# Diagonal sums of the recurrent heads: four 512-column products with a broadcast column of ones in place of eight 128-row blocks

## The chip, the core and the metric

The kernel runs on one core of one Trainium2 chip. The metric is the device time of one execution in microseconds (us). A core has a matrix engine (PE, with its weight loads shown apart as PEld), a vector engine (DVE), an activation engine (ACT), a general engine (POOL) and a queue engine that issues most transfers (SP). [...]

## The reference, cut to what matters

One decoder layer on 1024 tokens of width 1024. A projection feeds eight heads of dilated attention and four heads of a gated recurrence (HGRN2) of width 128; then follow the output projection and a feed-forward net of width 4096. The change lies in the recurrence, which the reference computes in chunks:

```python
qf = silu(q)                      # per head, (tokens, 128)
log_f = logaddexp(log(lb), log1p(-lb) + log_sigmoid(f_pre))
kf = -expm1(log_f)                # 1 - f
# in a chunk: b = cumsum(log_f)
a[t, s] = sum_k qc[t, k] * kc[s, k] * exp(b[t, k] - b[s, k])   # s <= t
o = o_inter + a @ vc
```

On the diagonal, s = t, the decay is one, and `a[t, t]` is the plain sum over the 128 channels of `qf * kf` at token t. These diagonal sums are what the changed lines compute.

## The kernel before, in words

Everything is held turned: channels on the 128 partitions, 1024 tokens along the free side. Where f32 exactness matters and speed too, a value is split in two fp32r parts (`hi` by an ACT copy, `lo = x - hi` by a DVE subtraction, `split_into` L82 to L84), and a product is done in three passes (`three_pass`, L86 to L89).

The order of the work is written by hand. A queue holds generators (projections of the next head, `hgrn_ig` L351 and `hgrn_qf` L368; in the last head the first attention projections, `attn_proj` L611). `fill(ns)` (L170) takes pieces from this queue until their stated costs have used up `ns`; so the instruction streams of all engines are a fixed weave of one head's recurrence (`hgrn_core`, L427) and the next head's projections. Debt is carried from one `fill` to the next. In front of each head's core the queue is drained.

`hgrn_qf(h)` makes, in two halves of 512 tokens, `qt` (silu of q), the forget gate `tot`, `kt` = 1 - f, and `prod = qt * kt` (L399), and then scales `qt` by `tot` (L400). DVE does these on L394 to L400, with sigmoids from ACT (L395, L396).

`hgrn_core(h)` for heads 0 to 2: `quarter_sets` (L403) makes query sets for the first step, by ACT copies (L414, L418) and DVE products (L419, L421). After `fill(3300)` come eight products `pd` (L434), one for each block of 128 tokens: the block of `prod` is the stationary operand, the column `ones` (128 x 1) the moving one, and the sums come out with tokens on the partitions, one column per block. DVE copies the 128 x 8 result (`dg`, L436) and multiplies it with the identity into `at` (L438), the matrix of diagonals that holds the scores of a head. After another `fill(1200)` come three steps. Each makes score products `pl` in four banks of the tags `s` and `t` (L451), rescales `qt`, `kt` and the totals on DVE (L464 to L478) while it makes the next query sets, and copies the scores into `at` under masks (`copy_predicated`, L483), which sets the four banks free; then `fill(7000)`. Then follow the transposed keys (`pk`), the state products (`pu`) and the outputs (`po`, two banks of the tag `pv`), and gate products of L573 that read `po`. Head 3 instead goes through seven levels, each with one bank of products `pl` (L512), DVE rescaling (L516, L518, L522) and one masked copy (L523), with fills of 2900 times 1.15.

In head 3 two things stand in front of the core (L1003 to L1005): the load of the first attention bias table, `load_bias(0)` (L691), and a dummy activation `texp` that makes ACT load its table for the exponential ahead of time. The rows of weights are split by `w_split` (L107), called as pieces of the queue are taken; its lines in the profile are L83 (ACT, `wh`) and L84 (DVE, `wl`).

Buffers go round in rings by tag: `S` nine slabs of 128 x 1024, `BT` two, `half` two of 128 x 512; in PSUM two banks each for `mm`, `s`, `t` and `pv`. `prod` was a slab of `S`, `pd` a bank of `t`. `BT` is used by the attention's bias tables and later by weights.

Of the kernel before, what the change touches and what calls it, by code (L numbers as in the profile page):

```python
# [8 lines left out]
F32 = mybir.dt.float32  # L9
F32R = mybir.dt.float32r  # L10
U8 = mybir.dt.uint8
AF = mybir.ActivationFunctionType
ALU = mybir.AluOpType
# [4 lines left out]
P = 128  # L18
# [3 lines left out]
NT = T // P  # L22
# [4 lines left out]
HH = 4  # L27
# [3 lines left out]
def f32(ap):  # L31
    return ap.bitcast(F32)
# [3 lines left out]
def hymba_layer(ctx, tc, x, w_in, w_out, w_ff1, w_ff2, g_pre, lb_logits, g_mix, g_post,  # L36
                g_mlp, g_mlp_post, bias_tab, level_masks, ident_in, fold_in, out):
    nc = tc.nc
    V, S, G, TE = nc.vector, nc.scalar, nc.gpsimd, nc.tensor

    ctx.enter_context(tc.manual_schedule())
    cp = ctx.enter_context(tc.tile_pool(name="consts", bufs=1))
# [7 lines left out]
    def slab(tag, name, dtype=F32, shape=(P, T)):  # L50
        return sp.tile(list(shape), dtype, tag=tag, name=name,
                       bufs={"S": 9, "T": 9, "P": 3, "BT": 2, "V8": 2, "R": 1}[tag])

    def bank(tag, name):
        return ps.tile([P, 512], F32, tag=tag, name=name,
                       bufs={"mm": 2, "s": 2, "t": 2, "pv": 2}[tag])

    def half(name, dtype=F32):
        return sp.tile([P, 512], dtype, tag="half", name=name, bufs=2)

    def col(name, n=1):
        return tp.tile([P, n], F32, tag=f"c{n}", name=name)

    ident = cp.tile([P, P], F32, name="ident")
# [3 lines left out]
    lbl = cp.tile([P, HH, 2], F32, name="lbl")  # L68
    lb = cp.tile([P, HH], F32, name="lb")
    omlb = cp.tile([P, HH], F32, name="omlb")  # L70
    ones = cp.tile([P, 1], F32, name="ones")
    nhalf = cp.tile([P, NT], F32, name="nhalf")
    rstd0 = cp.tile([P, NT], F32, name="rstd0")
    ssq0 = cp.tile([P, NT], F32, name="ssq0")
# [32 lines left out]
    def w_split(eng=V):  # L107
        i = done[1]
        if i < len(stream):
            if done[0] <= i:  # L110
                w_load()
            hl = stream[i][1]
            if hl is None:
                hl = (wp.tile([P, T], F32R, tag="wh", name=f"wh{i}", bufs=2),
                      wp.tile([P, T], F32R, tag="wl", name=f"wl{i}", bufs=2))
            else:
                hl = hl()
            split_into(hl[0], hl[1], raws.pop(i), eng)
            parts[i] = hl
            done[1] += 1  # L120
            w_load()

    def w_get(i, ahead=1):
        while done[1] < min(i + 1 + ahead, len(stream)):
            w_split()
        return parts[i]
# [43 lines left out]
    def fill(ns, least=False):  # L170
        debt[0] += ns
        if least:
            debt[0] = max(debt[0], 1.0)
        while debt[0] > 0 and queue:
            try:
                cost = next(queue[0])
            except StopIteration:
                queue.pop(0)
                continue
            if cost is None:  # L180
                break
            debt[0] -= cost
        debt[0] = min(debt[0], 0.0)

    def drain():
        while queue:
            n = len(queue)
            fill(1e9)
            assert len(queue) < n or not queue
# [20 lines left out]
    def x_load(t):  # L210
        nc.sync.dma_start(out=xrows[t], in_=x[t * P:(t + 1) * P, :])
# [5 lines left out]
    for c in range(2):  # L217
        sl = slice(c * 512, c * 512 + 512)
# [4 lines left out]
            nc.sync.dma_start(out=raws[i][:, sl], in_=stream[i][0][:, sl])  # L223
    for t in range(1, NT):
        x_load(t)
    V.memset(ones, 1.0)
    V.memset(nhalf, -0.5)
    rrow = slab("R", "rrow")
    mraw = slab("T", "mraw", F32, (P, len(LEVELS), 64))
# [46 lines left out]
    def row_scale(hf):  # L276
        sl = slice(hf * 512, hf * 512 + 512)
        pt = bank("t", f"rb{hf}")
        for j in range(4):
            t = hf * 4 + j  # L280
            TE.transpose(pt[:, j * P:(j + 1) * P], rstd0[:, t:t + 1].to_broadcast([P, P]), ident)
        S.activation(rrow[:, sl], pt, AF.Copy)
# [44 lines left out]
    for q in (2, 3):  # L327
# [7 lines left out]
                    in1=first.unsqueeze(2).to_broadcast([P, 3, 64]), op=ALU.mult)  # L335
# [5 lines left out]
    def proj_t(w, name, hf, out_box):  # L341
        wh, wl = kc(w[0]), kc(w[1])
        pm = bank("mm", f"pm_{name}{hf}")
        for k in range(NK):
            three_pass(pm, (wh[:, k], wl[:, k]), part(hT, k, hf), k == 0, k == NK - 1)
            out_box[0] = pm
            if k < NK - 1:
                yield 650.0
# [19 lines left out]
    def hgrn_qf(h):  # L368
        hd = heads[h]
        box = [None]  # L370
        w = w_get(4 * h + 2)
        hd["prod"] = slab("S", f"prod{h}")
        qt = hd["qt"] = slab("S", f"qt{h}")
        sig = slab("P", f"sig{h}")
        for hf in range(2):
            sl = slice(hf * 512, hf * 512 + 512)
            yield from proj_t(w, f"q{h}", hf, box)
            if h == 0:
                row_scale(hf)
            V.tensor_tensor(out=qt[:, sl], in0=box[0], in1=rrow[:, sl], op=ALU.mult)  # L380
            S.activation(sig[:, sl], qt[:, sl], AF.Sigmoid)
            V.tensor_tensor(out=qt[:, sl], in0=qt[:, sl], in1=sig[:, sl], op=ALU.mult)
            yield 650.0
        w = w_get(4 * h + 3, 0)
        kt = hd["kt"] = slab("S", f"kt{h}")
        tot = hd["tot"] = slab("S", f"tot{h}")
        for hf in range(2):
            sl = slice(hf * 512, hf * 512 + 512)
            for n, cost in enumerate(proj_t(w, f"f{h}", hf, box)):
                if hf == 0 and n == 3:  # L390
                    w_get(4 * h + 3, 2 if h + 1 < HH else 1)
                yield cost
            fr = half(f"fr{h}{hf}")
            V.tensor_tensor(out=fr, in0=box[0], in1=rrow[:, sl], op=ALU.mult)  # L394
            S.activation(tot[:, sl], fr, AF.Sigmoid)  # L395
            S.activation(kt[:, sl], fr, AF.Sigmoid, scale=-1.0)  # L396
            V.tensor_scalar(tot[:, sl], tot[:, sl], omlb[:, h:h + 1], lb[:, h:h + 1], op0=ALU.mult, op1=ALU.add)
            V.tensor_scalar(kt[:, sl], kt[:, sl], omlb[:, h:h + 1], None, op0=ALU.mult)
            V.tensor_tensor(out=hd["prod"][:, sl], in0=qt[:, sl], in1=kt[:, sl], op=ALU.mult)  # L399
            V.tensor_tensor(out=qt[:, sl], in0=qt[:, sl], in1=tot[:, sl], op=ALU.mult)  # L400
            yield 650.0

    def quarter_sets(hd, h, step, tots):  # L403
# [23 lines left out]
    def hgrn_core(h, scale, after=None):  # L427
        hd = heads[h]
        inat, gate, prod, qt, kt, tot = (hd[n] for n in ("inat", "gate", "prod", "qt", "kt", "tot"))
        ready = quarter_sets(hd, h, 0, tot) if h < HH - 1 else None  # L430
        fill(3300 * scale)
        pd = bank("t", f"pd{h}")
        for c in range(NT):
            TE.matmul(pd[:, c:c + 1], prod[:, c * P:(c + 1) * P], ones, start=True, stop=True)  # L434
        dg = col("dg", NT)
        V.tensor_copy(dg, pd[:, :NT])  # L436
        at = slab("S", f"at{h}", F32, (P, NT, P))
        V.tensor_tensor(out=at, in0=ident.unsqueeze(1).to_broadcast([P, NT, P]),  # L438
                        in1=dg.unsqueeze(2).to_broadcast([P, NT, P]), op=ALU.mult)
        if h < HH - 1:  # L440
            fill(1200 * scale)
            totals = slab("P", f"tot{h}")
            for step in range(3):
                c = 4 ** step
# [3 lines left out]
                for u in range(4):  # L448
                    pl = bank("st"[u // 2], f"pl{h}_{step}{u}").rearrange("p (n q) -> p n q", n=2)
                    for n in range(2 * u, 2 * u + 2):  # L450
                        TE.matmul(pl[:, n % 2, :192], kt[:, n * P:(n + 1) * P], sets[u // 2][:, n % 4],  # L451
                                  start=True, stop=True)
# [12 lines left out]
                for hf in range(2):  # L465
# [3 lines left out]
                                    in0=sets[hf][:, :, 128:].rearrange("p n (b w) -> p n b w", b=nb),  # L469
                                    in1=cv[:, n4, :, 0:1].to_broadcast([P, 4, nb, 2 * c]), op=ALU.mult)  # L470
# [19 lines left out]
            for n in range(NT):  # L490
                TE.matmul(pl[:64, n * 64:(n + 1) * 64], kt[:, n * P:n * P + 64], qt[:, n * P + 64:(n + 1) * P],
                          start=True, stop=True)
# [8 lines left out]
            fill(3400 * scale)  # L501
        else:
            cur = tot
            fill(1200 * scale)
            for li, c in enumerate(LEVELS):
                nb = 64 // c
                qv = qt.rearrange("p (b two c) -> p b two c", two=2, c=c)
# [3 lines left out]
                for n in range(NT):  # L511
# [5 lines left out]
                                in1=cv[:, :, 1:2].to_broadcast([P, w, c]), op=ALU.mult)  # L517
                V.tensor_tensor(out=qv[:, :, 1, :], in0=qv[:, :, 1, :],  # L518
                                in1=cv[:, :, 0:1].to_broadcast([P, w, c]), op=ALU.mult)
# [10 lines left out]
        for hf in range(2):  # L530
            pt = bank("t", f"pk{h}_{hf}")
            for j in range(4):
                n = hf * 4 + j
# [4 lines left out]
        for g4 in range(2):  # L538
            pu = bank("pv", f"pu{h}_{g4}")
            for j in range(min(4, NT - 1 - g4 * 4)):  # L540
                n = g4 * 4 + j
                TE.matmul(pu[:, j * P:(j + 1) * P], ktr[:, n], inat[:, n], start=True, stop=True)
            for j in range(min(4, NT - 1 - g4 * 4)):
                n = g4 * 4 + j
# [10 lines left out]
        for g4 in range(2):  # L555
            po = bank("pv", f"po{h}_{g4}").rearrange("p (n c) -> p n c", n=4)
            for j in range(4):
                n = g4 * 4 + j
# [132 lines left out]
    def load_bias(hd):  # L691
        if hd < AH and hd not in bts:
            bts[hd] = slab("BT", f"bt{hd}") if hd < AH - 1 else early["table"][:, 0]
            nc.sync.dma_start(out=bts[hd], in_=bias_tab[hd])
# [305 lines left out]
    for h in range(HH):  # L1000
        last = h == HH - 1
        queue += [attn_proj(0), attn_proj(1)] if last else [hgrn_ig(h + 1), hgrn_qf(h + 1)]
        if last:  # L1003
            load_bias(0)
            S.activation(col("texp"), nhalf[:, :1], AF.Exp)  # L1005
        hgrn_core(h, 1.15 if last else 1.0, open_attention if last else None)
        if not last:
            drain()
# [23 lines left out]
    for s in range(n_steps):  # L1032
        if s % 16 == 6:
            first_done[s // 16] = True
        hd, b = steps[s]
# [731 lines left out]
    scale, base = gpre, lbl.rearrange("p h l -> p (h l)")  # L1767
# [95 lines left out]
    for i in range(4):  # L1863
        t = 4 + i
# [100 lines left out]
```

## Time and profile before

| what | us |
|---|---|
| median of 3 runs (lowest, highest) | 1245.24 (1244.72, 1245.63) |
| the profiled execution | 1245.78 |
| its span, first to last instruction | 1244.0 |
| PE busy, 62 to 312 us (the four heads' cores) | 247.67 of 250 |
| DVE busy, same stretch | 179.64 |
| ACT busy, same stretch | 71.69 |
| POOL busy, same stretch | 15.26 |

The profile is of one execution. In its rows, a time is the start since the first instruction, then the duration, the engine, the line of the kernel, the operation, the output and its inputs, the shape, and in brackets the idle time ahead of it with whom it waited for. Matmuls are pipelined: the next one starts before the last has ended, so the distance between starts is what one costs. A plain-f32 matmul shows as two records: the eight products of one head are sixteen records.

### The profile page before, as it was taken

How to read it: one execution, taken by the hardware profiler on the slowest of the kernel's cores; microseconds unless marked ns; L12 is line 12 of the kernel's file. 1: busy time of each engine (PE TensorE's matmuls, PEld its weight loads, DVE VectorE, ACT ScalarE, POOL GpSimd, SP SyncE). 2: the span in 40 equal slices, each digit the busy share in tenths (PEclk: the TensorE clock that was granted, in tenths of full speed). 3: DMA queues.
4: the chain of work that ended last, by engine and by line, in shares of the span. 5: the costliest groups of instructions: out<-in, count | busy, mean ns of one | idle time of the engine just before them, and what ended most of it. 6: DMA issues, size and time to landing. Idle time of an engine off the chain costs nothing. (4 is left out here: it accounts for less than half of the span.)

```text
span 1244.0 us, 17240 instructions
## 1 busy us (share of the span) xinstructions
PE 1228.6 (99%) x6510; PEld 1051.1 (84%) x6510; DVE 865.3 (70%) x1490; ACT 543.4 (44%) x995; POOL 308.7 (25%) x304
## 2 busy tenths in 40 slices
PE   8999999999999999999999999999999999999998
PEld 8898989888888888888878788888888888888886
DVE  5686959584766667768769766676678645388795
ACT  7623232222655556665565322222225453444462
POOL 0000000020312123146250477557532000000022
PEclk9999999999999999999999999999999999999999
DMA  5201111121313233345342546455378624433337
GB/s 213 69 18 51 35 52 35 35 85 52 102 53 101 56 98 110 105 143 177 104 151 79 209 169 237 161 203 186 126 290 312 233 89 160 162 87 99 119 101 272
DMA packets 61138, 159.75 MB, mean 128 GB/s; under 512 B 5248, under 2 KB 13184, under 8 KB 61056
## 3 DMA queue, kind: packets, MB, share of 16 engines
q1 hardware_dynamic: 61056, 158.66, 37.9%
q8 instruction: 51, 0.84, 0.3%
q14 instruction: 31, 0.25, 0.1%
HBM read 110.40 MB, written 41.94 MB: 122 GB/s over the span
## 5 line engine op out<-in xcount | busy, mean ns | idle before, releaser
L84 DVE TENSOR_TENSOR al<-ar,ah 128x1024 fp32r<-128x1024 f32 x56 | 70.6, 1261 | 79.5 <-ACT ah L83 77.0
L1705 PE MATMUL f<-bh,al 128*128 128x512 f32 x320 | 124.5, 389 | 0.0
L1705 PE MATMUL f<-bh,ah 128*128 128x512 f32 x320 | 124.5, 389 | 0.0
L1705 PE MATMUL f<-bl,ah 128*128 128x512 f32 x320 | 124.5, 389 | 0.0
L83 ACT ACTIVATE ah<-ar 128x1024 fp32r<-128x1024 f32 x56 | 59.1, 1056 | 87.6 <-DMA ar<-actd 85.3
L1705 PEld LDWEIGHTS f<-bh,ah 128*128 128x128 f32 x320 | 60.1, 188 | 12.6
L1705 PEld LDWEIGHTS f<-bh,al 128*128 128x128 f32 x320 | 60.1, 188 | 12.6
L1705 PEld LDWEIGHTS f<-bl,ah 128*128 128x128 f32 x320 | 60.1, 188 | 12.3
L745 DVE TENSOR_TENSOR ptl<-pt,pth 128x512 fp32r<-128x512 f32 (+2 forms) x96 | 50.3, 552 | 20.0 <-ACT pth L744 19.9
L1779 POOL TENSOR_SCALAR lbl<-ssq 128x1 f32<-128x1 f32 x4 | 3.3, 818 | 244.4 <-ACT fd L1775 244.3
L744 ACT ACTIVATE pth<-pt 128x512 fp32r<-128x512 f32 (+2 forms) x96 | 43.3, 486 | 39.9 <-PE pt L741 38.7
L717 DVE CUSTOM_DVE_ANT_0 p<-ps,bt 128x512 f32<-128x512 f32 (+2 forms) x84 | 44.4, 553 | 22.1 <-PE ps L715 21.8
L1332 POOL TENSOR_TENSOR e<-x,e 128x512 f32<-128x512 f32 x14 | 21.5, 1539 | 134.1 <-DVE x L1283 134.1
L774 POOL TENSOR_TENSOR anat<-anat,rd 128x128 f32<-128x128 f32 x32 | 16.4, 512 | 150.0 <-DVE anat L773 147.4
L728 ACT ACTIVATE p<-p,nm 128x128 f32<-128x128 f32 (+3 forms) x64 | 49.5, 773 | 6.9 <-DVE nm L721 6.5
L79 POOL TENSOR_SCALAR ms<-hss 128x8 f32<-128x8 f32 x4 | 0.8, 197 | 199.9 <-DVE hss L564 199.8
L1705 PE MATMUL f2s<-bl,ah 128*128 128x512 f32 (+1 forms) x128 | 48.9, 382 | 0.0
L1705 PE MATMUL f2s<-bh,al 128*128 128x512 f32 (+1 forms) x128 | 48.9, 382 | 0.0
L1705 PE MATMUL f2s<-bh,ah 128*128 128x512 f32 (+1 forms) x128 | 48.9, 382 | 0.0
L741 PE MATMUL pt<-ident,p 128*128 128x128 f32 x288 | 42.7, 275 | 0.9 <-DVE ptl L745 0.7
L84 DVE TENSOR_TENSOR bl<-br,bh 128x1024 fp32r<-128x1024 f32 x32 | 40.1, 1253 | 1.3 <-ACT bh L83 1.2
L758 PE MATMUL pov<-pth,v 128*128 128x256 f32 (+1 forms) x160 | 40.3, 287 | 0.0
(1634 smaller groups left out, 3935.3 us busy)
## 6 DMA issues: line engine op xcount, KB each, us to landing
ar<-actd SPq DMA_DIRECT2D x56, 512.0 KB, 3.6
br<-in_w_ff_dram SPq DMA_DIRECT2D x16, 1024.0 KB, 6.2
w1r<-in_w_ff_dram SPq DMA_DIRECT2D x14, 1024.0 KB, 6.3
raw<-in_w_in_dram SPq DMA_DIRECT2D x26, 512.0 KB, 3.5
actd<-e SPq DMA_DIRECT2D x17, 768.0 KB, 4.1
actd<-e SPq DMA_DIRECT2D x11, 1024.0 KB, 4.0
raw<-in_w_out_dram SPq DMA_DIRECT2D x8, 512.0 KB, 3.6
xres<-in_x_dram SPq DMA_DIRECT2D x8, 512.0 KB, 4.2
```

Source lines behind the costliest of these rows:

```text
L83: S.activation(hi, src, AF.Copy)
L84: eng.tensor_tensor(out=lo, in0=src, in1=f32(hi), op=ALU.subtract)
L717: V.tensor_tensor_reduce(out=pe[:, k0:k0 + n], in0=pS[:, :n], in1=bts[hd][:, o:o + n], scale=1.0, scalar=-3.0e38, op0=ALU.add, op1=ALU.max ...
L728: S.activation(pe[:, :nk], pe[:, :nk], AF.Exp, bias=nm[:, b:b + 1], accum_out=dn[:, b:b + 1])
L741: TE.transpose(pt[:, j * P:(j + 1) * P], pe[:, jj * P:(jj + 1) * P], ident)
L744: S.activation(hi, src, AF.Copy)
L745: V.tensor_tensor(out=lo, in0=src, in1=f32(hi), op=ALU.subtract)
L758: TE.matmul(po[:, c0:256], vst, pt[j // 4][q][:, j % 4, c0:], start=j == 0 and q == 0, stop=j == nj - 1 and q == 1)
L774: G.tensor_tensor(out=dst, in0=dst, in1=stats[hd]["rd"][:, b].unsqueeze(2).to_broadcast([P, 2, 64]), op=ALU.mult)
L1332: eng[0].tensor_tensor(out=e1[:, 3], in0=a21, in1=e1[:, 2], op=ALU.add)
L1705: TE.matmul(pm, a[:, j, c], b[:, j, d], start=start and j == 0 and q == 0, stop=stop and j == 1 and q == 2, skip_group_check=True)
L1779: G.tensor_scalar(base[:, t:t + 1], sums[j][:, t:t + 1], 1.0 / D, EPS, op0=ALU.mult, op1=ALU.add)
```

## The change

The stationary and the moving operand change places: the column of ones, broadcast to 128 x 128, is loaded as weights, and the product runs past it as 512 moving columns. Each row of the bank then holds the same 512 sums, and the identity picks the diagonal out of it. So that this runs in fp32r, the product is split: `full` in f32 (a `half` buffer), `prod[0]` its ACT copy in fp32r, `prod[1]` the rest by a DVE subtraction; the bank takes two passes. Per head there are four matmuls of 512 columns in place of eight of one column, two ACT copies and two DVE subtractions more, two diagonal products of 128 x 512 on DVE that read PSUM in place of one of 128 x 1024 and a small copy. `prod` moves from one slab of `S` to both of `BT`, `pd` from a bank of `t` to the two of `pv`. The two fills become one of 4500 ahead of the products. The load of the first bias table moves behind the products of head 3, since it takes a `BT` slab.

```diff
-    ones = cp.tile([P, 1], F32, name="ones")
+    ones = cp.tile([P, 1], F32R, name="ones")
...
-    V.memset(ones, 1.0)
+    V.memset(f32(ones), 1.0)
...
     def hgrn_qf(h):
-        hd["prod"] = slab("S", f"prod{h}")
...
         w = w_get(4 * h + 3, 0)
+        hd["prod"] = prod = [slab("BT", f"pr{q}{h}", F32R) for q in "hl"]
         kt = hd["kt"] = slab("S", f"kt{h}")
...
             V.tensor_scalar(kt[:, sl], kt[:, sl], omlb[:, h:h + 1], None, op0=ALU.mult)
-            V.tensor_tensor(out=hd["prod"][:, sl], in0=qt[:, sl], in1=kt[:, sl], op=ALU.mult)
+            full = half(f"pr{h}{hf}")
+            V.tensor_tensor(out=full, in0=qt[:, sl], in1=kt[:, sl], op=ALU.mult)
+            S.activation(prod[0][:, sl], full, AF.Copy)
             V.tensor_tensor(out=qt[:, sl], in0=qt[:, sl], in1=tot[:, sl], op=ALU.mult)
+            V.tensor_tensor(out=prod[1][:, sl], in0=full, in1=f32(prod[0][:, sl]), op=ALU.subtract)
             yield 650.0
...
     def hgrn_core(h, scale, after=None):
-        fill(3300 * scale)
-        pd = bank("t", f"pd{h}")
-        for c in range(NT):
-            TE.matmul(pd[:, c:c + 1], prod[:, c * P:(c + 1) * P], ones, start=True, stop=True)
-        dg = col("dg", NT)
-        V.tensor_copy(dg, pd[:, :NT])
+        fill(4500 * scale)
         at = slab("S", f"at{h}", F32, (P, NT, P))
-        V.tensor_tensor(out=at, in0=ident.unsqueeze(1).to_broadcast([P, NT, P]),
-                        in1=dg.unsqueeze(2).to_broadcast([P, NT, P]), op=ALU.mult)
+        for hf in range(2):
+            pd = bank("pv", f"pd{h}_{hf}")
+            for q in range(2):
+                TE.matmul(pd, ones.to_broadcast([P, P]), prod[q][:, hf * 512:hf * 512 + 512], start=q == 0, stop=q == 1)
+            V.tensor_tensor(out=at[:, hf * 4:hf * 4 + 4], in0=ident.unsqueeze(1).to_broadcast([P, 4, P]),
+                            in1=pd.rearrange("p (n c) -> p n c", n=4), op=ALU.mult)
+        if h == HH - 1:
+            load_bias(0)
         if h < HH - 1:
-            fill(1200 * scale)
             totals = slab("P", f"tot{h}")
...
         else:
             cur = tot
-            fill(1200 * scale)
             for li, c in enumerate(LEVELS):
...
         if last:
-            load_bias(0)
             S.activation(col("texp"), nhalf[:, :1], AF.Exp)
```

## The prediction

> **What bounds the kernel now.** I read the page first, then the waits of the recurrent heads, then the timelines of the engines around the changed lines. The page's engine lines (busy time, share of the span, instructions):
>
> ```profile
> span 1244.0 us, 17240 instructions
> PE 1228.6 (99%) x6510; PEld 1051.1 (84%) x6510; DVE 865.3 (70%) x1490; ACT 543.4 (44%) x995; POOL 308.7 (25%) x304
> ```
>
> PE is busy for 99% of the span, so at first sight any PE time removed comes off the end. But this is a mean over stages. The windows view gives head 1's stretch from the last projection to the end of its second set of score products (columns: window, length, then busy us of PE, PEld, DVE, ACT, POOL):
>
> ```profile
> 125.20:146.50 21.30, 20.35 (x154) 19.39 (x154) 19.59 (x45) 6.86 (x20) 0.00 (x0) 1.00 0.16 50
> ```
>
> There DVE is busy 19.59 of 21.30 us, nearly as much as PE. The waits of 40 to 320 us (total, times, longest) say who waits:
>
> ```profile
> DVE kt L476 <- PE pl L451: 6.8, 3, 2.3
> ...
> PEld pl L451 <- DVE at L483: 4.7, 8, 0.6
> ```
>
> PE's weight loads for `pl` wait eight times for the masked copies of L483, which free the score banks. In the third step of each head it is DVE that waits for PE (L476, three times, up to 2.3 us): PE is the later one again by then, so what DVE costs PE in step 1 is neither won back nor paid a second time. The PEld timeline of head 1:
>
> ```profile
> 128.72 1.88 PEld L434 LDWEIGHTS pd<-ones,prod 128*128 128x128 f32 x16
> 130.52 0.19 PEld L87 LDWEIGHTS pig<-wig2h,hTh 128*128 128x128 f32 x1
> ...
> 131.94 2.59 PEld L451 LDWEIGHTS pl<-qs,kt 128*128 128x128 f32 x16
> ...
> 145.90 0.62 PEld L451 LDWEIGHTS pl<-qs,kt 128*128 128x128 f32 x4 [0.61 <-DVE at L483]
> ```
>
> The diagonal products occupy PE from 128.72 to 130.52, 1.80 us. PE's last bank of step 1 starts at 145.90 only because DVE has just finished with it. The DVE timeline that leads there:
>
> ```profile
> 119.92 0.69 DVE L564 TENSOR_REDUCE hss<-ysq 128x4 f32<-128x512 f32 x1 [2.43 <-ACT ysq L563]
> ...
> 123.67 0.69 DVE L400 TENSOR_TENSOR qt<-qt,tot 128x512 f32<-128x512 f32 x1
> 124.28 2.15 DVE L573 SCALAR_TENSOR_TENSOR gate<-po,hrs,gate 128x128 f32<-128x128 f32 x8
> 126.35 0.68 DVE L394 TENSOR_TENSOR fr<-pm_f,rrow 128x512 f32<-128x512 f32 x1
> ...
> 128.77 0.69 DVE L399 TENSOR_TENSOR prod<-qt,kt 128x512 f32<-128x512 f32 x1
> 129.50 0.69 DVE L400 TENSOR_TENSOR qt<-qt,tot 128x512 f32<-128x512 f32 x1
> 130.11 0.38 DVE L419 TENSOR_TENSOR qs<-qt,tot 128x128 f32<-128x128 f32 x1
> ...
> 131.43 0.43 DVE L421 TENSOR_TENSOR qs<-qs,tot 128x256 f32<-128x256 f32 x1
> 131.97 1.23 DVE L84 TENSOR_TENSOR wl<-raw,wh 128x1024 fp32r<-128x1024 f32 x1
> 133.11 0.16 DVE L436 COPY dg<-pd 128x8 f32<-128x8 f32 x1
> ...
> 134.45 0.62 DVE L464 TENSOR_TENSOR qt<-qt,tot 128x256 f32<-128x256 f32 x1
> ...
> 145.41 0.44 DVE L483 COPY_PREDICATED at<-near,pl 128x128 f32<-128x128 uint8 x1
> ```
>
> DVE starts this chain when PE lets it (the 2.43 us wait for `ysq`, whose source is PE's `po`), and from there to 145.85 it has no gap but short ones in which ACT works for it. So between those two points time is DVE's chain, not PE's sum. The last masked copy ends at 145.41 + 0.44 = 145.85, and PE's bank starts 0.05 later.
>
> **The change part by part.** PE first. Pitch, not duration, is what a matmul costs in a stream; here is one of the projection, fp32r, 512 columns:
>
> ```profile
> 59.27 0.39 PE L87 MATMUL pm_f<-hTh,wh 128*128 128x512 f32 x1
> 59.50 0.39 PE L88 MATMUL pm_f<-hTl,wh 128*128 128x512 f32 x1
> ```
>
> Four new ones per head cost 4 x 0.23 = 0.9 us for the 1.8 us removed: PE saves 0.9 us per head, 3.6 us in four. The weight load of a broadcast column I take as hidden behind the stream, as the other loads are; it can be no dearer than the loads it replaces, since there are four and not sixteen.
>
> DVE and ACT next. The split adds, per half, one ACT copy and one DVE subtraction. The nearest rows have their very shapes:
>
> ```profile
> L83 ACT ACTIVATE wf<-s 128x512 fp32r<-128x512 f32 x14 | 8.7, 621 | 1.3 <-POOL e L1334 1.2
> ```
> ```profile
> L84 DVE TENSOR_TENSOR wig0l<-raw,wig0h x4: 683/692/693, 6.3 to 10.9; 128x512 fp32r<-128x512 f32 x4
> ```
>
> The copy (0.62) runs beside the scaling of `qt` (0.69), so the subtraction starts some 0.06 us after `qt` and then pushes what follows by its pitch of 0.61 (129.50 to 130.11): 0.67 us per half. The diagonal itself gets slightly cheaper: column copy and product took 133.11 to 134.45 = 1.34; two 128x512 products at 0.61 are 1.22, so -0.12. Before L84 DVE idles a little (131.43 + 0.43 = 131.86 to 131.97), since ACT's `wh` is not there:
>
> ```profile
> 130.89 1.04 ACT L83 ACTIVATE wh<-raw 128x1024 fp32r<-128x1024 f32 x1
> ```
>
> ACT is delayed by about as much as DVE, less the second half's copy being over early, so I let that 0.11 be given back.
>
> Heads 1 and 2: the first half's subtraction stands ahead of the eight gate products of L573, and L394 starts right behind those (124.28 + 2.07), so 0.67 passes through; the second half adds 0.67. Sum 1.34 - 0.12 - 0.11 = **+1.1 us each** at 145.85, hence at PE. The 0.9 us that PE saves before it is spent waiting in step 1. PE meets new waits on the way, the `pl` of step 0 among them (its operands from L421 come 1.3 later, about 0.4 us after PE gets there), but these hide in the same wait.
>
> Head 0: the first half costs nothing, because DVE waits there for PE:
>
> ```profile
> 62.87 0.69 DVE L394 TENSOR_TENSOR fr<-pm_f,rrow 128x512 f32<-128x512 f32 x1 [1.51 <-PE pm_f L89]
> ```
>
> That leaves 0.67 - 0.12, about **+0.5**. Head 3 has no quarter steps and works level by level. ACT's, DVE's, POOL's and PEld's timelines:
>
> ```profile
> 255.11 1.28 ACT L1005 ACT_TABLE_LOAD   x1
> 256.40 0.20 ACT L1005 ACTIVATE texp<-nhalf 128x1 f32<-128x1 f32 x1
> 256.51 1.04 ACT L83 ACTIVATE wh<-raw 128x1024 fp32r<-128x1024 f32 x1
> ```
> ```profile
> 255.65 0.69 DVE L399 TENSOR_TENSOR prod<-qt,kt 128x512 f32<-128x512 f32 x1
> ...
> 261.32 0.69 DVE L516 TENSOR_TENSOR kt<-kt,tot 128x512 f32<-128x512 f32 x1 [0.57 <-PE pl L512]
> 261.93 1.78 DVE L518 TENSOR_TENSOR qt<-qt,tot 128x512 f32<-128x512 f32 x1
> ```
> ```profile
> 261.49 3.37 POOL L629 TENSOR_TENSOR ql<-qf,q 64x512 fp32r<-64x512 f32 x2 [11.66 <-ACT q L628]
> ```
> ```profile
> 255.98 1.98 PEld L434 LDWEIGHTS pd<-ones,prod 128*128 128x128 f32 x16
> 259.16 1.98 PEld L512 LDWEIGHTS pl<-qt,kt 128*128 128x128 f32 x16
> 265.06 1.98 PEld L512 LDWEIGHTS pl<-qt,kt 128*128 128x128 f32 x16
> ```
>
> The second half's product moves to 256.32, its ACT copy runs 257.05 to 257.65, and the table load, which stood right behind the sigmoids, now stands behind that copy: `wh` ends at about 260.05 instead of 257.55. DVE waits for it, then does `wl` (1.14), the attention query's evacuation (0.61), two diagonal products (1.22): L516 starts at 263.1 instead of 261.32. PE has two more projection steps before `pd` (six matmuls at 0.23, to 257.35), waits there for the second half's subtraction (257.7 to 258.4), starts the first `pl` at 258.7 instead of 259.16 and would reach the second at 264.6 instead of 265.06. It needs L518. With L516 and L518 at 0.61 and 1.70, as before, that is 265.4. But POOL's subtractions move with the evacuation to about 262.7 to 266.0, and what DVE runs beside them took 1.78 instead of 0.69; now L516 is caught as well, and L518 ends near 266.3. I take 266.3, **+1.2** for PE; the bounds are -0.9 (no wait at all) and +1.5 (both at full 1.78).
>
> Moved buffers: `prod` leaves S for BT, idle until the bias tables, and the bias load now waits for `pd`, behind the next weight load in SP's queue. Its first use is in the attention stage, after all seven levels of head 3; queued behind it are the copies of the query's low part, which wait for POOL's L629 anyway: nothing. The two `pv` banks of `pd` are free once L573 ends (126.4), ahead of 128.72: nothing; were that cover gone, the wait would again fall in DVE's shadow.
>
> Sum: 0.5 + 1.1 + 1.1 + 1.2 = +3.9 us. The profiled execution took 1245.78 us, 1.78 around its span, and would take 1249.7; it lies 0.54 above the median of the three runs, 1245.24, on which the forecast stands: **1249.1 us**.
>
> [...]
>
> **Rivals.** *A, faster: PE is the bound everywhere.* DVE has a hole in each half, while ACT makes the sigmoid (eight halves):
>
> ```profile
> DVE tot L397 <- ACT tot L395: 5.6, 8, 0.7
> ```
>
> If the new work falls into such holes and the chain gets shorter, PE keeps 0.9 x 4: 1245.24 - 3.6 = 1241.6. It decides once the last copy of step 1 comes 0.9 us sooner than now. For it: 99% PE. Against: the eight waits on L483, and a DVE queue that runs in order, so that a subtraction can't slide back into a hole. [...]
>
> *B, about the same: head 3 gains.* If the table load slips ahead, or POOL doesn't hold L516 up, head 3 gives 0 to -0.9 and the total is 2.7 - 0.5 = +2.2: 1247.4.
>
> *C, a hold behind the table load* as long as the load itself (1.28): head 3 is 1.3 later, 1250.4.
>
> *D, the new products aren't fast.* Were they run at the plain-f32 rate of `pl` (2.59 us for eight of 192 columns, 0.86 per 512), four would take 3.5 us, 1.7 more than those removed. Heads 0 to 2 would hide nearly all of it in step 1's wait, head 3 not: about 1251. Against it: both operands are fp32r, as in the projection.
>
> **How the numbers follow.** Forecast 0.55, A 0.13, B 0.22, C 0.05, D 0.05. About 0.2% (2.5 us) is what a measurement of this kernel can tell from no change: faster is A, 0.13; same is B, 0.22; slower is the rest, 0.65. The forecast's own range is 1247.8 to 1249.8: head 3 between +0.2 and +1.5, heads 0 to 2 between 2.4 and 3.1 (five subtractions at 0.61, or at 0.69 + 0.06). Upward the range goes to 1250.6 to take in C; downward it goes past B to 1244.3, where DVE's chain would be neither longer nor shorter and head 3 had its 0.9; it leaves out A, and D's upper part.
>
> **What would show it.** In the changed profile: four `pd` matmuls per head some 0.23 apart (else D); L483's waits by L451 longer, and in heads 0 to 2 from the first bank on (else A); the second `pl` of head 3 waiting for L518, with L516 near 1.7 us (else B). I am wrong if PE reaches step 1 after DVE, or if the ACT copy is so late that DVE stands still for it.

## The result and the profile after

| | median, us | runs | lowest to highest |
|---|---|---|---|
| before | 1245.64 | 6 | 1244.72 to 1246.05 |
| changed | 1250.78 | 6 | 1248.93 to 1251.35 |

The ratio is 1.0044, with a 95% interval of 1.0034 to 1.0054: the change makes the kernel slower by some 5.1 us. The forecast, 1249.1, had the direction; the measured time lies 0.2 us above the upper end of its range, 1250.6. The profiled execution took 1250.63, with a span of 1248.8.

The page of the changed kernel, engine lines and the row of the clock that PE was granted (tenths, 40 slices):

```profile
span 1248.8 us, 17160 instructions
PE 1230.5 (99%) x6462; PEld 1049.8 (84%) x6462; DVE 865.8 (69%) x1498; ACT 548.3 (44%) x1003; POOL 307.9 (25%) x304
...
PEclk9999999989999999999999999999999999999999
```

PE is busy for 1.9 us more, though its work per head became shorter; and in the ninth slice, about 250 to 281 us, where head 3 lies, the clock row has an 8. Before the change it had none. The waits of 40 to 330 us:

```profile
PEld pl L454 <- DVE at L486: 6.9, 12, 0.6
...
PEld pl L514 <- issue: 1.9, 1, 1.9
...
PE pl L514 <- DVE qt L520: 1.6, 1, 1.6
```

PE's weight loads now wait twelve times, not eight, for the masked copies (L486 is the old L483), and there is a new wait, nearly two us in one piece, at the second level of head 3 (L514 is the old L512). PEld of head 1, the same rows as in the prediction:

```profile
129.95 0.19 PEld L439 LDWEIGHTS pd<-prh,ones 128*128 128x128 f32 x1
130.07 0.19 PEld L439 LDWEIGHTS pd<-prl,ones 128*128 128x128 f32 x1
130.64 0.18 PEld L439 LDWEIGHTS pd<-prh,ones 128*128 128x128 f32 x1 [0.38 <-ACT prh L401]
131.36 0.18 PEld L439 LDWEIGHTS pd<-prl,ones 128*128 128x128 f32 x1 [0.54 <-DVE prl L403]
132.19 2.57 PEld L454 LDWEIGHTS pl<-qs,kt 128*128 128x128 f32 x16 [0.65 <-DVE qs L424]
142.96 0.62 PEld L454 LDWEIGHTS pl<-qs,kt 128*128 128x128 f32 x4 [0.56 <-DVE at L486]
...
146.65 0.62 PEld L454 LDWEIGHTS pl<-qs,kt 128*128 128x128 f32 x4 [0.61 <-DVE at L486]
```

The four products cost no more than their place in the stream where nothing holds them up (in head 0 they start at 67.17, 67.41, 67.63 and 67.87), but here PE waits for their operands, for the query sets behind them, and then from the first bank of step 1 on. DVE of head 1:

```profile
119.71 0.69 DVE L566 TENSOR_REDUCE hss<-ysq 128x4 f32<-128x512 f32 x1 [2.43 <-ACT ysq L565]
...
123.46 0.69 DVE L402 TENSOR_TENSOR qt<-qt,tot 128x512 f32<-128x512 f32 x1
124.13 0.69 DVE L403 TENSOR_TENSOR prl<-pr,prh 128x512 fp32r<-128x512 f32 x1
124.73 2.15 DVE L575 SCALAR_TENSOR_TENSOR gate<-po,hrs,gate 128x128 f32<-128x128 f32 x8
...
132.90 1.22 DVE L84 TENSOR_TENSOR wl<-raw,wh 128x1024 fp32r<-128x1024 f32 x1
134.03 1.28 DVE L440 TENSOR_TENSOR at<-ident,pd 128x512 f32<-128x512 f32 x2
135.23 0.62 DVE L467 TENSOR_TENSOR qt<-qt,tot 128x256 f32<-128x256 f32 x1
```

From DVE's start (L564, now L566) to PE's last bank of step 1 it was 145.90 - 119.92 = 25.98 us; now it is 146.65 - 119.71 = 26.94: **+0.96**. This measure, DVE's start to PE's last bank in head 1, is used for every kernel below. Set side by side instruction by instruction, the two traces give +0.25 for head 0 and +0.94 for head 2. Head 3, by ACT, DVE, POOL and PEld, in this order:

```profile
258.75 0.63 ACT L401 ACTIVATE prh<-pr 128x512 fp32r<-128x512 f32 x1 [1.28 <-DVE pr L400]
259.40 1.28 ACT L1006 ACT_TABLE_LOAD   x1
260.69 0.20 ACT L1006 ACTIVATE texp<-nhalf 128x1 f32<-128x1 f32 x1
260.80 1.04 ACT L83 ACTIVATE wh<-raw 128x1024 fp32r<-128x1024 f32 x1
```
```profile
261.88 1.23 DVE L84 TENSOR_TENSOR wl<-raw,wh 128x1024 fp32r<-128x1024 f32 x1 [1.77 <-ACT wh L83]
...
264.81 1.48 DVE L518 TENSOR_TENSOR kt<-kt,tot 128x512 f32<-128x512 f32 x1
266.21 1.75 DVE L520 TENSOR_TENSOR qt<-qt,tot 128x512 f32<-128x512 f32 x1
```
```profile
264.44 2.97 POOL L631 TENSOR_TENSOR ql<-qf,q 64x512 fp32r<-64x512 f32 x2 [13.25 <-ACT q L630]
```
```profile
260.27 1.98 PEld L514 LDWEIGHTS pl<-qt,kt 128*128 128x128 f32 x16
...
268.08 2.67 PEld L514 LDWEIGHTS pl<-qt,kt 128*128 128x128 f32 x16 [1.95 <-issue]
...
276.39 1.98 PEld L514 LDWEIGHTS pl<-qt,kt 128*128 128x128 f32 x16
```

This is the forecast chain to the step: the table load behind the copy, the weights' split behind the load, L518 and L520 slowed beside POOL, PE waiting 1.95 us. But then the third level starts 8.31 us after the second, where before the change it was 5.24 (265.06 to 270.30):

```profile
270.30 1.87 PEld L512 LDWEIGHTS pl<-qt,kt 128*128 128x128 f32 x15
```

The windows view around that place shows why (the last numbers are granted clock, share and rate of transfers):

```profile
262.00:269.00 7.00, 5.45 (x30) 4.40 (x30) 7.00 (x8) 1.26 (x2) 2.89 (x2) 1.00 0.39 107
269.00:275.80 6.80, 6.80 (x22) 5.74 (x22) 4.20 (x6) 1.31 (x3) 0.66 (x1) 0.50 0.28 83
275.80:283.00 7.20, 7.20 (x47) 6.41 (x46) 3.92 (x6) 1.00 (x1) 1.89 (x2) 1.00 0.24 43
```

PE's clock was **halved for 6.8 us**, right after the wait, and PE did 22 matmuls there where the next 7.2 us hold 47. That cost 3.1 to 3.3 us, and the forecast has no such term. Together, instruction against instruction in the two profiled executions: -0.46 at the start of the program (the first transfers), +0.25, +0.96, +0.94, +1.13 in the heads, +3.26 by the clock, and -1.26 behind them (at the start of the attention and of the feed-forward, where the other execution waited): 4.82, the difference of the spans.

The 6.8 us hold for the profiled execution, whose mean granted clock is 0.996. By themselves they bring the mean over 1249 us down to 0.9973. Four of the other five runs (1250.30 to 1251.35) show 0.998 and the one of 1248.93 shows 0.999, so in these the clock was down for a shorter time or not at all. What each of them lost by it was not traced.

### The profile page after: what moved, and what is told of

Read it like the earlier page. It is cut to its first block, busy times and chain, and to the rows that moved or that the text cites. A ratio compares the mean times of both kernels' runs of the same rounds, so it can differ in the third digit from the quotient of the medians.

```text
span 1248.8 us, 17160 instructions
## 1 busy us (share of the span) xinstructions
PE 1230.5 (99%) x6462; PEld 1049.8 (84%) x6462; DVE 865.8 (69%) x1498; ACT 548.3 (44%) x1003; POOL 307.9 (25%) x304
## 5 line engine op out<-in xcount | busy, mean ns | idle before, releaser
L84 DVE TENSOR_TENSOR al<-ar,ah 128x1024 fp32r<-128x1024 f32 x56 | 70.6, 1261 | 79.9 <-ACT ah L83 77.7
L84 DVE TENSOR_TENSOR bl<-br,bh 128x1024 fp32r<-128x1024 f32 x32 | 40.1, 1253 | 1.1 <-ACT bh L83 1.0
```

Source lines behind the costliest of these rows:

```text
L84: eng.tensor_tensor(out=lo, in0=src, in1=f32(hi), op=ALU.subtract)
```

## The experiments

The theory: in heads 0 to 2 DVE's chain, with ACT's part of it, sets when step 1 ends, and PE's work there counts for nothing; in head 3 a delayed split makes PE wait, and the wait halves the clock. The rivals: PE's sum counts; the lower clock belongs to the kind of work in the changed heads; the new products themselves are dear. Each kernel was timed in turn with the kernel before on the same chip; the medians of before were 1244.52 for e1 to e4, 1244.79 for e6 with four copies and 1244.81 for the rest. The times expected of e1 to e4 were reckoned from the 1245.64 of the result, so they are best read as differences from it.

**e1_texp_later.** The changed kernel, with the dummy exponential moved:

```diff
+        if h == HH - 1:
             load_bias(0)
+            S.activation(col("texp"), nhalf[:, :1], AF.Exp)
...
-        if last:
-            S.activation(col("texp"), nhalf[:, :1], AF.Exp)
```

> The changed kernel, with the dummy exponential of head 3 (and so the activation table load) issued behind the diagonal products instead of ahead of the core; nothing else is different. Theory 1 (chain and clock): in head 3 the weights' ACT split no longer stands behind the 1.28 us load, DVE's chain ends about 1.4 us sooner, PE's 1.95 us wait at the second level goes to 0.3 or less, and the half clock that followed it (6.8 us, some 3.3 us lost) does not come. Heads 0 to 2 keep their +0.3, +0.95, +0.95. Time 1246.2 to 1247.6. Theory 2 (the lower clock comes from the kind of work in the changed heads, not from the wait): the clock still falls, time 1249.5 or more. Theory 3 (the new products themselves cost PE more than those they replace): 1250 and no change in heads 0 to 2.

Measured: 1246.88 (1246.22 to 1247.91), ratio 1.0018 (1.0009 to 1.0027). Head 3's second level:

```profile
266.62 1.53 PEld L515 LDWEIGHTS pl<-qt,kt 128*128 128x128 f32 x13 [0.46 <-issue]
```

The wait fell from 1.95 to 0.46 us, where 0.3 or less was foreseen, and the clock was 1.00 throughout:

```profile
262.00:268.00 6.00, 5.93 (x34) 4.89 (x34) 6.00 (x7) 2.75 (x4) 2.92 (x2) 1.00 0.60 142
268.00:275.00 7.00, 7.00 (x43) 6.16 (x43) 4.80 (x8) 2.32 (x3) 2.15 (x2) 1.00 0.17 66
```

So about half of the 5.1 us hung on where one 1.28 us load stands in ACT's queue. Heads 0 to 2 kept their price (+0.41, +0.93, +0.94), and head 3 gains 0.36. What is left, 2.4 us, is somewhat more than the 0.6 to 2.0 expected; the next run takes it apart.

**e2_no_low.** As e1, without the low part: the DVE subtraction and the second pass are taken out.

```diff
-            V.tensor_tensor(out=prod[1][:, sl], in0=full, in1=f32(prod[0][:, sl]), op=ALU.subtract)
...
-            for q in range(2):
-                TE.matmul(pd, ones.to_broadcast([P, P]), prod[q][:, ...], start=q == 0, stop=q == 1)
+            TE.matmul(pd, ones.to_broadcast([P, P]), prod[0][:, ...], start=True, stop=True)
```

> As e1_texp_later, but the low part of the product is left out: no DVE subtraction and one pass instead of two for each bank of diagonal sums, so the sums are only fp32r-exact. Per head PE has 0.45 us less than with both passes, 1.35 less than before the change; DVE's chain is about 0.1 to 0.2 us shorter than before the change. Theory 1 (DVE's chain sets the end of step 1 in heads 0 to 2): these heads end 0.1 to 0.3 us sooner than before, PE's saving turns into wait, and only head 3 gives its 1.35. Time 1243.4 to 1244.4. Rival A of the prediction (PE's sum is the bound everywhere): 4 x 1.35 = 5.4 us off, 1240.2.

Measured: 1244.26 (1243.57 to 1245.57), ratio 0.9996 (0.9987 to 1.0005). With 5.4 us less PE work than before the change, the time is the same within the noise: rival A is refuted. But the theory's number was missed too: -0.3 us against before, where -1.2 to -2.2 was expected. In the heads ACT's half of the chain is the reason. Head 1:

```profile
130.18 0.43 DVE L423 TENSOR_TENSOR qs<-qs,tot 128x256 f32<-128x256 f32 x1 [0.31 <-ACT qs L420]
...
131.77 1.23 DVE L84 TENSOR_TENSOR wl<-raw,wh 128x1024 fp32r<-128x1024 f32 x1 [0.33 <-ACT wh L83]
```

Without its subtraction DVE waits twice for ACT, which has the copy to do first. Head 1's measure is 145.52 - 119.29 = 26.23, +0.25 and not -0.2. By these two waits it is the ACT copy that costs it, although no run has the copy alone; the two subtractions of head 1 cost the other 0.7.

**e3_no_products.** The kernel before, without the diagonal products.

```diff
-        pd = bank("t", f"pd{h}")
-        for c in range(NT):
-            TE.matmul(pd[:, c:c + 1], prod[:, c * P:(c + 1) * P], ones, start=True, stop=True)
-        V.tensor_copy(dg, pd[:, :NT])
+        V.tensor_copy(dg, prod[:, :NT])
```

> The kernel before, with the eight diagonal products of each head left out: the column copy reads eight columns of the product slab instead, so the diagonals are wrong and PE has 1.8 us less work per head while DVE has the same work. Theory 1: heads 0 to 2 end step 1 at the same time as before, PE waiting up to 1.8 us more for the masked copies; only head 3 gives 1.8. Time 1243.8, and up to 3.4 us more for each head in which that wait, now 1.8 us in one piece, halves the clock. Rival A (PE's sum): 7.2 us off, 1238.4.

Measured: 1242.75 (1242.63 to 1245.54), ratio 0.9987 (0.9979 to 0.9996), 1.8 us off. Head 1, DVE and PEld:

```profile
119.95 0.69 DVE L561 TENSOR_REDUCE hss<-ysq 128x4 f32<-128x512 f32 x1 [2.43 <-ACT ysq L560]
```
```profile
131.11 2.57 PEld L448 LDWEIGHTS pl<-qs,kt 128*128 128x128 f32 x16 [0.85 <-DVE qs L421]
142.18 0.62 PEld L448 LDWEIGHTS pl<-qs,kt 128*128 128x128 f32 x4 [0.85 <-DVE at L480]
...
145.88 0.62 PEld L448 LDWEIGHTS pl<-qs,kt 128*128 128x128 f32 x4 [0.61 <-DVE at L480]
```

The measure is 25.93, as before the change (25.98), with 1.8 us of PE work gone: PE waits 0.85 and 0.85 instead. Only head 3 gives its 1.8. This is the plainest proof that in heads 0 to 2 no saving on PE can be seen. The waits were split in two, and the clock stayed (mean 0.999 in the profiled execution, as in that of before).

The profiled execution of e3 is the slowest of its eleven, 1245.54. Against the profile of before it lost 1.7 us far behind the heads, in the feed-forward, where the split of a weight came late; below are the wait, the stretch of 3.41 us that holds nearly all of it, and the next:

```profile
640.07 0.19 PEld L1263 LDWEIGHTS f13a<-h2h,wa3l 128*128 128x128 f32 x1 [2.00 <-DVE wa3l L84]
```
```profile
636.55:639.96 3.41, 1.96 (x8) 1.05 (x6) 2.21 (x1) 3.27 (x5) 3.25 (x3) 1.00 0.13 54
639.96:643.37 3.41, 3.30 (x14) 2.74 (x15) 3.10 (x3) 1.88 (x3) 3.41 (x3) 1.00 0.00 0
```

So PE's weight loads waited 2.00 us in one piece here, and the clock stayed at 1.00 behind it. That bears on the theory of head 3 and is taken up below.

**e4_head3_only.** The old lines in heads 0 to 2, the new ones in head 3; the edit is the change itself, kept to the last head:

```diff
+        new = h == HH - 1
+        if not new:
+            hd["prod"] = slab("S", f"prod{h}")
...
+        if new:
+            hd["prod"] = prod = [slab("BT", f"pr{q}{h}", F32R) for q in "hl"]
...
+            if new:
+                S.activation(prod[0][:, sl], full, AF.Copy)
```

> The kernel before in heads 0 to 2 and the changed kernel in head 3 alone. Theory 1: head 3 waits as in the changed kernel, 1.5 to 2 us at the second level, and the clock halves for about 6.8 us: +1.1 and +3.3, less what the start of the attention gives back (0.8): 1248.7 to 1249.7. Theory 2 (the clock falls for what heads 0 to 2 did, the wait is not enough): about +1.1, 1246.7. Rival A: -0.9, 1244.7.

Measured: 1247.24 (1245.06 to 1249.11), ratio 1.0020 (1.0011 to 1.0028): between the two theories, with runs spread over four us, from next to no loss to the whole of it. Its profiled execution, of 1249.11, waited 1.93 us at the second level, and the clock fell, for one stretch of 3.4 us:

```profile
264.90:268.30 3.40, 1.86 (x15) 1.43 (x13) 3.40 (x4) 0.00 (x0) 1.55 (x1) 1.00 0.37 92
268.40:271.80 3.40, 3.40 (x13) 2.92 (x13) 2.50 (x5) 0.00 (x0) 0.00 (x0) 0.50 0.49 149
271.80:275.00 3.20, 3.20 (x21) 2.79 (x19) 1.29 (x2) 1.83 (x3) 1.17 (x1) 1.00 0.02 5
```

Heads 0 to 2 are not needed for it. The forecast of a full 6.8 us in every run was wrong. The runs' mean clocks go with their times: 0.998 in the five from 1247.74 to 1249.11, 0.999 in the six from 1245.06 to 1247.24.

**e6_late_by_3, e6_late_by_4, e6_late_by_5.** Nothing of the change: the kernel before, with idle ACT copies ahead of head 3's core (three, four, five), which delay the split of the weights and so make a wait of a chosen length.

```diff
             S.activation(col("texp"), nhalf[:, :1], AF.Exp)
+            idle = slab("P", "idle")
+            for _ in range(5):
+                S.activation(idle, rrow, AF.Copy)
```

> The kernel before with three idle ACT copies of 128x1024 (about 2.9 us) ahead of head 3's core, which only delay the split of the weights in head 3. By head 3's timeline this makes PE wait at its second level for about 2.9 - 2.0 = 0.9 us. Theory 1: that wait is paid once and the clock stays: 1244.5 + 0.9 = 1245.4. If the clock's fall belonged to any wait at this place: 1247 to 1249.

> As e6_late_by_5 with four copies. With five, PE waited 2.3 us at the second level and the clock halved for 6.8 us; with three it did not wait at all. Four should make it wait 1.1 to 1.4 us. [...]

> As e6_late_by_3 with five copies (about 4.8 us), nothing of the changed kernel in it: PE waits about 2.8 us at the second level. Theory 1 (the wait itself halves the clock): the clock falls to a half for one or two stretches of 3.4 us: 1244.5 + 2.8 + 1.7 to 3.4 = 1249.0 to 1250.7, in nearly every run. Theory 2 (the kind of work in the changed lines makes it fall): 1247.3 with a clock of 1.00 throughout.

Measured: with three 1244.94, ratio 0.9998 (0.9990 to 1.0007); with four 1246.16, 1.0012 (1.0003 to 1.0021); with five 1250.48 (1247.57 to 1251.32), 1.0036 (1.0022 to 1.0050). The second level of each, in this order (with three it has no wait: the 0.9 us foreseen was wrong, since POOL now came at 264.44 us, too late to slow L516 and L518, 0.68 and 0.69 us long):

```profile
264.94 1.92 PEld L512 LDWEIGHTS pl<-qt,kt 128*128 128x128 f32 x16
```
```profile
265.64 1.53 PEld L512 LDWEIGHTS pl<-qt,kt 128*128 128x128 f32 x13 [1.20 <-DVE qt L518]
```
```profile
267.24 2.71 PEld L512 LDWEIGHTS pl<-qt,kt 128*128 128x128 f32 x16 [2.29 <-DVE qt L518]
```

And the clock with five:

```profile
268.00:275.00 7.00, 7.00 (x24) 5.94 (x23) 5.51 (x7) 1.31 (x3) 2.58 (x3) 0.51 0.17 40
```

A wait of 2.29 us, in a kernel that has none of the changed lines, halves the clock for 6.8 us in the profiled execution, and the median is 5.7 us above before; the three slowest runs have a mean clock of 0.996 to 0.997, the others 0.998 (1248.90) and 0.999 (1247.57). With a wait of 1.20 the kernel costs 1.4 us, about what the wait lasts, and the clock stays (mean 0.999 in the profiled execution). Theory 2 is refuted: at this place it is the wait, and not the changed lines.

**e7_low_on_pool.** As e1, with the subtraction on POOL.

```diff
-            V.tensor_tensor(out=prod[1][:, sl], in0=full, in1=f32(prod[0][:, sl]), op=ALU.subtract)
+            G.tensor_tensor(out=prod[1][:, sl], in0=full, in1=f32(prod[0][:, sl]), op=ALU.subtract)
```

> As e1_texp_later, with the subtraction of the split moved from DVE to POOL (about 1.3 us for 128x512 in rows of the later stages). If DVE's own two subtractions are the cost in heads 0 to 2, and POOL beside it were free, this falls to the time of e2_no_low plus 0.45 for head 3: 1244.7. If POOL holds DVE up while both read (the 1.78 us rows of head 3), what DVE runs beside it takes some 1.0 longer per half and nothing or little is won: 1246.5 to 1248.

Measured: 1246.47 (1245.76 to 1247.55), ratio 1.0014 (1.0006 to 1.0023). Head 1, DVE and POOL:

```profile
130.68 1.12 DVE L424 TENSOR_TENSOR qs<-qs,tot 128x256 f32<-128x256 f32 x1 [0.32 <-ACT qs L421]
```
```profile
130.08 1.43 POOL L403 TENSOR_TENSOR prl<-pr,prh 128x512 fp32r<-128x512 f32 x1 [4.60 <-ACT prh L401]
```

The product that runs beside POOL takes 1.12 us where it took 0.43. Of the 0.7 that the subtractions cost in head 1, 0.3 is won (its measure is 146.28 - 119.65 = 26.63, against 26.94), the other 0.4 stays, in the main by this product.

**e5_diag_on_act.** The other way round: the products of before are kept, and DVE's chain is made shorter by what ACT can do.

```diff
-        V.tensor_copy(dg, pd[:, :NT])
+        S.activation(dg, pd[:, :NT], AF.Copy)
...
-        V.tensor_tensor(out=at, in0=ident.unsqueeze(1).to_broadcast([P, NT, P]),
-                        in1=dg.unsqueeze(2).to_broadcast([P, NT, P]), op=ALU.mult)
+        for n in range(NT):
+            S.activation(at[:, n], ident, AF.Copy, scale=dg[:, n:n + 1])
```

> The kernel before with its one-column products kept, but the column copy and the diagonal product moved from DVE to ACT: one copy of 128x8 and eight scaled copies of the identity, one per block. Nothing else differs; PE has the same work as before. Theory 1 (DVE's chain up to the last masked copy of step 1 sets PE's time in heads 0 to 2): the chain loses 1.34 us per head, PE's waits of step 1 shrink from 1.8 to about 0.5, heads 1 and 2 end 1.3 sooner and head 0 about 1.0: 1244.5 - 3.6 = 1240.9, somewhat later if ACT's nine operations (some 2.3 us behind the weights' split) hold up its next query sets. Rival A (PE's sum is the bound): nothing moves, 1244.5.

Measured: **1241.56** (1240.67 to 1242.40), ratio 0.9972 (0.9962 to 0.9982): faster than both kernels, by 3.3 us against before where 3.6 was expected. Head 1, ACT and PEld:

```profile
131.17 2.45 ACT L439 ACTIVATE at<-ident,dg 128x128 f32<-128x128 f32 x8
133.52 0.40 ACT L414 ACTIVATE qs<-qt 128x256 f32<-128x256 f32 x1
```
```profile
141.24 1.94 PEld L451 LDWEIGHTS pl<-qs,kt 128*128 128x128 f32 x12
143.73 0.62 PEld L451 LDWEIGHTS pl<-qs,kt 128*128 128x128 f32 x4 [0.55 <-DVE at L483]
```

ACT does the diagonal in a time in which it had nothing to do (before, it stood idle for 3.50 us from 131.93 on); of the three waits of step 1 one is left. The measure is 143.73 - 119.06 = 24.67, 1.31 less than before, with the same work on PE.

## Why the prediction went wrong, point by point

- **What bounds the kernel.** Right, and shown from both sides: PE work taken away in heads 0 to 2 gives next to nothing (0.13 us or less a head, e3), DVE work taken away gives 1.3 us or a little more in heads 1 and 2 and 0.8 in head 0 (e5).
- **PE's saving.** The four products run at the pitch of 0.23 us that was taken, and in heads 0 to 2 the saving turned into waits. Rival D is out; rival A is refuted by e2 and e3.
- **Heads 0 to 2.** Forecast +0.5, +1.1, +1.1; measured +0.25, +0.96, +0.94. The terms are as worked out: each subtraction pushes what follows by 0.66 (123.46 to 124.73, less the old 0.61), 0.67 foreseen, and the diagonal takes 1.20 instead of 1.22. What was sized too small is the time that DVE no longer waits for ACT: the query sets up to L84 take 1.67 us (131.23 to 132.90) where they took 1.86 (130.11 to 131.97), so 0.19 is given back, not 0.11, and in head 0, where nothing was put down for it, 0.20. ACT's copy is hidden only beside the subtraction: without the subtraction head 1 is 0.25 longer (e2).
- **Head 3, the wait.** Forecast +1.2, measured +1.13, by the chain as told; e1 shows that it is the table load's place.
- **Head 3, the price of that wait: the step that failed.** The prediction put PE's wait down at its own length, "+1.2 for PE; the bounds are -0.9 (no wait at all) and +1.5 (both at full 1.78)". A wait of nearly two us in one piece was also followed by half the clock, for 6.8 us in the profiled execution, and that was another 3.3. With it the sum is 0.25 + 0.96 + 0.94 + 1.13 + 3.3 = 6.6, less what later waits took back (1.3 in the profiled execution), near the 5.1 measured. The take-back stands in the forecast no more than the clock does, and the two partly cancel: that the forecast came within 1.7 us of the measured time is in part luck. The trace of before could not price it, since no wait there was longer than 0.6 us in the heads and the clock row was flat; but that made it an unknown to be bounded from both sides, not a zero.
- **Rivals B and C.** B has the price of e1 (+2.4 us, where B had +2.2), whose table load does stand behind the split; as the kernel stood it did not happen. C, a hold behind the table load, did not either: `texp` starts 0.01 us behind it. The upper end of the range, 1250.6, was set to take in C, and no run shows such a hold.

Two things stay open. The first is when the clock falls and for how long: in e4's profile for 3.4 us, in other runs of e4 by their mean clock (0.999) not at all, in the changed kernel's profile for 6.8. The waits ahead of these two falls are nearly the same, 1.93 and 1.95 us, and no run shows what makes one fall twice as long as the other.

The second is which waits count. At head 3's second level waits of 1.93, 1.95 and 2.29 us were followed by the fall and one of 1.20 was not; but e3's wait of 2.00 us, in the feed-forward, was not either, so the length alone does not decide. PE's busy time was nearly the same in both cases: 1.85 us in the stretch from 265.60 to 269.00 of the changed kernel and 1.86 in the 3.40 us of e4, each just ahead of the fall, and 1.96 in the 3.41 us that hold nearly all of e3's wait. The matmuls beside the wait differ too, 64 columns at head 3's levels and 512 in the feed-forward. No run tells these apart.

## What to carry to other kernels

Before taking work off the engine that is busy for 99% of the span, follow one stage backwards from its last wait: in these heads the chain ran through DVE, PE's waits were at most 0.6 us each and easily overlooked, and in heads 0 to 2 a shorter PE bought next to nothing (0.13 us or less a head for 1.8, e3) while a longer DVE was paid nearly in full. When an added operation stands ahead of a table load or a long copy in an engine's queue, follow that queue to the next engine that waits for it: here one load of 1.28 us, moved behind the diagonal products, took PE's wait from 1.95 to 0.46 us (e1). And a wait on PE should not be priced at its length alone: once it is near two us in one piece (here 1.93 to 2.29), look at the granted clock behind it, in more than one execution.

## What the runs showed of the hardware

- A single wait of 1.93 to 2.29 us of PE's weight loads, at head 3's second level, was followed by 3.4 or 6.8 us at half clock (the changed kernel, e4, e6 with five). One of 1.20 there was not (e6 with four), nor were four of 0.6 to 0.85 at a distance of 1.2 us (head 1, the changed kernel and e3), nor one of 2.00 in the feed-forward (e3).
- A DVE product of SBUF operands that started while POOL subtracted took 1.48 to 1.78 us instead of 0.69 (128x512, head 3; before, L518 and L522; changed, L518 and L520), or 1.12 instead of 0.43 (128x256; e7). One that was already running kept its time (before, L516 at 261.32, 0.69), and so did one that started in the last 0.2 us of a subtraction (before, L516 at 272.45, 0.70).
- Matmuls of 512 columns against a broadcast column of ones ran at the pitch of ordinary ones (0.23 us, head 0 of the changed kernel), with weight loads of 0.19 us as usual.
